# Norm factors and bank scaling ahead in the order, attention scores as 64-row products, and 14 operand tiles, in a four-layer decoder kernel

## The chip, the cores and the metric

The kernel runs as one program on one core of a Trainium2 chip. The metric is device microseconds for one execution. TensorE (PE in the rows, its weight loads PEld) does the products, VectorE (DVE) and ScalarE (ACT) the work on elements, GpSimd (POOL) a few additions and fills, and SyncE (SP) issues the transfers. Weights come from HBM in transfers of 1 MB and are used once.

## The reference

The input is one sequence of 256 tokens with 1024 features. Four layers each add three sublayers to it: a feed-forward, a mixer, a feed-forward. The mixer is differential attention in layers 0 and 3, a recurrence (RWKV-7) in layer 1 and attention with a window of 128 tokens in layer 2. Cut to what matters here:

```
for i in range(DEPTH):                      # 4
    sh1, sc1, g1, sh2, sc2, g2, sh3, sc3, g3 = split(silu(c) @ ada_w[i] + ada_b[i])
    h = rms_norm(x, norm_g[i, 0]) * (1 + sc1) + sh1
    x = x + 0.5 * g1 * swiglu(h, ffn_w_in[i, 0], ffn_w_out[i, 0])     # 1024 -> 2 x 2816 -> 1024
    h = rms_norm(x, norm_g[i, 1]) * (1 + sc2) + sh2
    x = x + g2 * mixer(h)
    h = rms_norm(x, norm_g[i, 2]) * (1 + sc3) + sh3
    x = x + 0.5 * g3 * swiglu(h, ffn_w_in[i, 1], ffn_w_out[i, 1])
# attention of both kinds: heads of 64 features
q = rms_norm(q, q_norm_g); k = rms_norm(k, k_norm_g)
s = einsum(q, k) * 64 ** -0.5, masked
```

In differential attention 8 heads hold two score maps each; with the window, 16 query heads share 2 key heads, and two query heads are worked at a time.

## The kernel before

Activations lie with features on the 128 partitions and tokens along the row, so x is 8 tiles of 128x256. Every large product is made of three products of parts (`mm3`): weights and activations are split into a high part (`hi`) and a remainder (`lo`); line 287 multiplies high by high, 288 high weights by the activations' remainder, 289 the weights' remainder by high activations. `load` takes a 1 MB weight unit and splits it in 4 chunks: ACT casts `hi` (line 269), DVE subtracts `lo` (line 271). Beside this DVE works out the modulation vectors of later sublayers in pieces (`ada_unit`, line 344).

The instructions are handed to a scheduler that places them in one fixed order for each engine, by priority (what is written earlier comes earlier) and by its estimate of what is ready. At run time each engine goes through its order and waits where an operand or a buffer is missing.

**From one sublayer to the next.** `residual` writes a feature tile of x (line 577); `stat_add` adds up squares for the norm, and `pre` makes `xh`, the tile times its modulation scale but without the norm factor, split in two parts like every operand. `first_units` (line 519) lets PE begin with products of `xh`: a column of modulation shifts is appended to it, so that a bank of PSUM then holds the raw product in its columns 0 to 255 and the shift's product in column 256. A feed-forward does so for three weight units in six banks (tags a, d, b, two each), differential attention for three units in a, b, c, the window's attention for two in a, b. Meanwhile `rsqrt` (line 385) makes the norm factor `rsq` on DVE: a transpose (393), small steps of a Newton iteration (402 to 418), a transpose back (424). It is also used for the norms of q and k and of the heads' outputs, where the second transpose (`fin`) is called later. Then `make_h` makes the eight normalised operands `h`: `xr` (DVE, line 511), the high part (ACT, 513), the remainder (DVE, 514). `unraw` (line 536) finishes a bank of the raw start: ACT copies the shift's column, DVE multiplies the bank by `rsq` (line 541) and so frees it. `xh` and `h` share one ring of 10 tiles (tag h of pool `hp`), of which 8 hold `xh` until PE is through with them.

PSUM has two banks for each of the tags a, b, c, d. In a feed-forward, the unit after the raw ones goes to banks d and the next to a, so PE needs both freed.

**Scores.** `scores` (line 764) fills two banks for a head (or for two query heads of the window), c = 0 and 1. A mask product writes the bank (line 776), then queries 0 to 127 against keys 0 to 127 (777) and queries 128 to 255 against all 256 keys (779) are added. The two maps of a head lie on partitions 0 to 63 and 64 to 127 of q and k. Each product takes all 128 partitions: q is held twice in a padded tile `qp`, once with the lower and once with the upper half zero. The zeros are written once (`zero_tiles`), the 64 rows by two ACT instructions for each head (lines 906 and 1027), which also multiply by the q norm's gain. Keys are multiplied by the k norm's gain and norm factor (line 911, in the window 1071). There are 24 calls of `scores`: 8 in each differential layer and 8 in the window's.

Of the kernel before, what the change touches and what calls it, by code (L numbers as in the profile page):

```python
# [19 lines left out]
P = 128  # L20
# [208 lines left out]
class Trunk:  # L229
    def __init__(self, tc, ctx, aps, plan):  # L230
# [6 lines left out]
        self.hp = e(tc.tile_pool(name="hp", bufs=10))  # L237
# [147 lines left out]
    def rsqrt(self, ps, n, scale, eps, pool, floor=None, later=False, more=None):  # L385
# [41 lines left out]
        return fin if later else fin()  # L427
# [175 lines left out]
    def ffn(self, l, s):  # L603
# [4 lines left out]
        with ExitStack() as c:  # L608
# [16 lines left out]
            for j in range(first, NPAIR + 1):  # L625
                if j == 5:
                    self.load_rest()
                if j < NPAIR:
# [7 lines left out]
                    g = hp.tile([P, 2, 2, T], F32R, tag="g", bufs=NFIRST + 1 if first else 2, name=self.n("g"))  # L636
# [65 lines left out]
    def first_pairs(self, l, s, hp):  # L702
# [7 lines left out]
        for kp in range(4):  # L710
# [20 lines left out]
            for i in range(2):  # L731
# [5 lines left out]
                for k, j, f, c in todo:  # L737
# [8 lines left out]
                    if kp == 3 and (k, f, c) == (1, 1, 1):  # L746
                        gs[2 * i + j] = self.glu(hp, *banks[2 * i + j], bufs=NFIRST + 1)
# [16 lines left out]
    def scores(self, qp, kn, window):  # L764
# [5 lines left out]
        banks = []  # L770
        for c in range(2):
            ps = self.ps("a")
            b3 = ps[:, :384].rearrange("p (b k) -> p b k", b=3)
            mk = self.msk[:, P:].rearrange("p (b k) -> p b k", b=3)
            st = 1 if window else 2
            nc.tensor.matmul(b3[:, ::st], self.msk[:, :P], mk[:, ::st], start=True, stop=False, skip_group_check=True)
# [84 lines left out]
    def diff(self, l):  # L861
# [4 lines left out]
        with ExitStack() as c:  # L866
            mp = c.enter_context(self.tc.tile_pool(name=self.n("da"), bufs=2))
            qpads = self.zero_tiles(mp, [P, 2, T], "qp", 3)
# [25 lines left out]
            def head(h, qs, ks, raw):  # L894
                if raw:
                    sb = mp.tile([P, 512], F32, tag="qk", bufs=2, name=self.n("qk"))
# [618 lines left out]
```

## Time and profile before

| | |
|---|---|
| median of 3 runs | 2309.99 us (2307.81 to 2311.01) |
| the profiled execution's own time | 2310.26 us |
| its span, first to last instruction | 2308.4 us |
| mean granted TensorE clock | 0.974 |
| PE busy | 2193.9 us, 95% |
| PEld busy | 2104.0 us, 91% |
| DVE busy | 1766.9 us, 77% |
| ACT busy | 1196.4 us, 52% |

The profiled execution lies 0.27 us above the median and has 1.9 us outside its span. Windows give for a stretch of the span each engine's busy time and instructions, and the granted clock: 1.00 is 2.4 GHz, 0.50 is 1.2 GHz, a value between them a mixture of both. A timeline lists an engine's instructions with their start; equal neighbours stand as one row with a count (x3). The duration of a matmul overlaps the next one's, so what a matmul costs in a row of them is the distance between starts.

### The profile page before, as it was taken

What the parts mean: (1) busy time and instruction counts of PE and PEld (TensorE: products, weight loads), DVE (VectorE), ACT (ScalarE), POOL (GpSimd) and SP (SyncE); (2) the same over time, 40 slices, a digit from 0 to 9 for tenths busy, and PEclk for the clock granted to TensorE, in tenths of its full rate; (3) what the DMA queues carried; (4) which work ended last, traced back from release to release, by engine and by line L of the source; (5) the groups of instructions that cost most, each with busy time, mean ns of one, the idle gap of its engine ahead of it and who ended that gap; (6) DMA issues with size and microseconds to landing.
All of it is one profiled execution on the core that took longest, in us unless ns stands there. A gap on an engine that the chain in (4) does not pass through costs nothing.

```text
span 2308.4 us, 47699 instructions
## 1 busy us (share of the span) xinstructions
PE 2193.9 (95%) x19244; PEld 2104.0 (91%) x19244; DVE 1766.9 (77%) x4001; ACT 1196.4 (52%) x2675; POOL 112.7 (5%) x213
## 2 busy tenths in 40 slices
PE   7999899999999899888999999999999999999999
PEld 6999898999999687677999899888999999889999
DVE  6877999888855776767888965778889855999653
ACT  3545766445444474445444644586445444766442
POOL 0001001001000300001000100101001000101000
PEclk8999999999999998899999999999999999999999
DMA  8885456887754420026788665436888755554552
GB/s 341 357 330 207 176 190 243 341 328 289 277 183 183 148 74 2 21 74 239 285 317 329 261 249 183 157 146 231 338 321 305 282 183 183 185 190 158 201 183 74
DMA packets 72365, 505.90 MB, mean 219 GB/s; under 512 B 8016, under 2 KB 10448, under 8 KB 11600
## 3 DMA queue, kind: packets, MB, share of 16 engines
q1 hardware_dynamic: 71568, 502.20, 57.6%
q8 instruction: 151, 2.47, 0.4%
q10 hardware_dynamic: 576, 0.66, 0.1%
q14 instruction: 70, 0.57, 0.1%
HBM read 501.78 MB, written 1.05 MB: 218 GB/s over the span
## 4 chain that ended last, share of the span: by engine, by line
PE 45%; DVE 5%; ACT 1%; issue 1%; POOL 0%; DVEq 0%; ACTq 0%; POOLq 0%
PE psa L287 4%; PE psa L289 4%; PE psa L288 4%; PE psd L287 4%; PE psd L289 4%; PE psd L288 4%; PE psb L288 3%; PE psb L287 3%; PE psb L289 3%; PE psc L288 2%; PE psc L289 2%; PE psc L287 2%; DVE lo L271 2%; DVE x L577 1%; DVE xh L490 1%
## 5 line engine op out<-in xcount | busy, mean ns | idle before, releaser
L269 ACT CAST hi<-raw 128x512 fp32r<-128x512 f32 x1306 | 731.3, 618 | 720.2 <-issue 553.5
L271 DVE TENSOR_TENSOR lo<-raw,hi 128x512 fp32r<-128x512 f32 x1306 | 847.3, 691 | 240.2 <-ACT hi L269 239.3
L287 PE MATMUL psa<-h,hi 128*128 128x256 f32 x1336 | 377.7, 283 | 29.3 <-DVE sil L541 23.8
L289 PE MATMUL psa<-h,lo 128*128 128x256 f32 x1336 | 377.3, 282 | 0.0
L288 PE MATMUL psa<-h,hi 128*128 128x256 f32 x1336 | 376.8, 282 | 0.0
L287 PE MATMUL psd<-h,hi 128*128 128x256 f32 x1256 | 359.0, 286 | 0.0
L289 PE MATMUL psd<-h,lo 128*128 128x256 f32 x1256 | 359.0, 286 | 0.0
L288 PE MATMUL psd<-h,hi 128*128 128x256 f32 x1256 | 358.4, 285 | 0.0
L344 DVE SCALAR_TENSOR_TENSOR ada<-ada,cb 128x1024 f32<-128x1024 f32 x232 | 276.3, 1219 | 27.1 <-DMA ada<-in_ada_dram 27.1
L287 PEld LDWEIGHTS psa<-h,hi 128*128 128x128 f32 x1336 | 255.0, 191 | 31.1 <-ACT hi L269 17.3
L288 PEld LDWEIGHTS psa<-h,hi 128*128 128x128 f32 x1336 | 253.0, 189 | 0.2
L289 PEld LDWEIGHTS psa<-h,lo 128*128 128x128 f32 x1336 | 252.9, 189 | 0.0
L287 PEld LDWEIGHTS psd<-h,hi 128*128 128x128 f32 x1256 | 243.7, 194 | 0.7
L288 PEld LDWEIGHTS psd<-h,hi 128*128 128x128 f32 x1256 | 242.4, 193 | 0.7 <-issue 0.7
L289 PEld LDWEIGHTS psd<-h,lo 128*128 128x128 f32 x1256 | 242.0, 193 | 0.3
L289 PE MATMUL psb<-g,lo 128*128 128x256 f32 x704 | 199.3, 283 | 0.0
L287 PE MATMUL psb<-g,hi 128*128 128x256 f32 x704 | 199.3, 283 | 0.0
L288 PE MATMUL psb<-g,hi 128*128 128x256 f32 x704 | 199.2, 283 | 0.0
L288 PE MATMUL psc<-g,hi 128*128 128x256 f32 x704 | 199.0, 283 | 0.0
L289 PE MATMUL psc<-g,lo 128*128 128x256 f32 x704 | 199.0, 283 | 0.0
L287 PE MATMUL psc<-g,hi 128*128 128x256 f32 x704 | 198.9, 283 | 0.0
L289 PEld LDWEIGHTS psb<-g,lo 128*128 128x128 f32 x704 | 135.0, 192 | 0.0
(373 smaller groups left out, 4464.4 us busy)
## 6 DMA issues: line engine op xcount, KB each, us to landing
raw<-in_ffi_dram SPq DMA_DIRECT2D x175, 1024.0 KB, 4.9
ada<-in_ada_dram SPq DMA_DIRECT2D x116, 1024.0 KB, 7.3
raw<-in_ffo_dram SPq DMA_DIRECT2D x88, 1024.0 KB, 4.9
raw<-in_ada_dram SPq DMA_DIRECT2D x24, 1024.0 KB, 4.8
raw<-in_daqk_dram SPq DMA_DIRECT2D x16, 1024.0 KB, 4.8
raw<-in_rwr_dram SPq DMA_DIRECT2D x12, 1024.0 KB, 4.8
raw<-in_ff_dram SPq DMA_DIRECT2D x8, 1024.0 KB, 9.6
raw<-in_dav_dram SPq DMA_DIRECT2D x8, 1024.0 KB, 4.8
```

Of the source, the lines that this page charges most:

```text
L269: nc.scalar.copy(hi[:, sl], raw[:, sl])
L271: eng.tensor_tensor(lo[:, sl], raw[:, sl], hi[:, sl].bitcast(F32), op=ALU.subtract)
L287: nc.tensor.matmul(out, whi, ahi, start=start, stop=False, skip_group_check=True)
L288: nc.tensor.matmul(out, whi, alo, start=False, stop=False, skip_group_check=True)
L289: nc.tensor.matmul(out, wlo, ahi, start=False, stop=stop, skip_group_check=True)
L344: nc.vector.scalar_tensor_tensor(wk, wk, 1.0, self.cond, op0=ALU.mult, op1=ALU.mult, accum_out=raw[:, k:k + 1])
L490: nc.vector.scalar_tensor_tensor(h[:, 1, :T], self.x[d], a[:, d:d + 1], h[:, 0, :T].bitcast(F32), op0=ALU.mult, op1=ALU.subtract)
L577: nc.vector.scalar_tensor_tensor(t, acc[d // 2][:, (d % 2) * T:(d % 2 + 1) * T], gate[:, d:d + 1], self.x[d], op0=ALU.mult, op1=ALU.add)
```

## The change

It has four parts.

1. `rsqrt` and its `fin`, and the two instructions of `unraw`, are issued under `tc.high_priority()`: the scheduler places them ahead of other work that is ready.
2. `scores` takes q without padding. The product of map c uses partitions 64c to 64c + 63 of q and of the keys, so each product is 64 rows deep. The order in which they are written is: mask 0, mask 1, the two products of 128 keys, the two of 256 keys. The gain of q goes into the keys (`qkg`, one product of two vectors for each layer). The padded tiles, their fills and the two ACT copies for each head go. Where q came out of a raw bank (3 of 8 heads in a differential layer, 2 of 8 calls in the window's) the tile `qk` is used as it is; elsewhere one ACT copy of 128x256 takes it out of PSUM. `qk` has 3 buffers in the differential layers in place of 2.
3. The ring of tag h has 14 tiles in place of 10.
4. The ring of tag g in the program's first feed-forward has NFIRST tiles in place of NFIRST + 1 (NFIRST counts the pairs of hidden blocks with which the program begins).

```diff
-        self.hp = e(tc.tile_pool(name="hp", bufs=10))
+        self.hp = e(tc.tile_pool(name="hp", bufs=14))
...
-    def rsqrt(self, ps, n, scale, eps, pool, floor=None, later=False, more=None):
+    def rsqrt(self, *args, later=False, **kw):
+        with self.tc.high_priority():
+            fin = self._rsqrt(*args, **kw)
+        def done():
+            with self.tc.high_priority():
+                return fin()
+        return done if later else done()
+    def _rsqrt(self, ps, n, scale, eps, pool, floor=None, more=None):
...
-        nc.scalar.copy(b, bank[:, T:T + 1])
-        nc.vector.tensor_tensor(out, bank[:, :T], self.rs, op=ALU.mult)
+        with self.tc.high_priority():
+            nc.scalar.copy(b, bank[:, T:T + 1])
+            nc.vector.tensor_tensor(out, bank[:, :T], self.rs, op=ALU.mult)
...
-        banks = []
+        banks = [self.ps("a") for _ in range(2)]
+        b3 = [ps[:, :384].rearrange("p (b k) -> p b k", b=3) for ps in banks]
...
         for c in range(2):
...
-            nc.tensor.matmul(ps[:, 0:128], qp[:, c, 0:128], kn[:, 0:128], start=False, stop=True,
-                             skip_group_check=True)
-            nc.tensor.matmul(ps[:, 128:384], qp[:, c, 128:256], kn, start=False, stop=True, skip_group_check=True)
-            nc.vector.tensor_reduce(m3[:, c], b3, axis=AX.X, op=ALU.max)
-            banks.append(ps)
+            nc.tensor.matmul(b3[c][:, ::st], self.msk[:, :P], mk[:, ::st], start=True, stop=False, skip_group_check=True)
+        for qs, ks in ((slice(0, P), slice(0, P)), (slice(P, T), slice(0, T))):
+            for c in range(2):
+                r = slice(c * 64, c * 64 + 64)
+                os = slice(0, P) if qs.start == 0 else slice(P, 3 * P)
+                nc.tensor.matmul(banks[c][:, os], q[r, qs], kn[r, ks], start=False, stop=True, skip_group_check=True)
...
-                qp = qpads[h % 3]
-                for cc in range(2):
-                    ps_ = slice(cc * 64, cc * 64 + 64)
-                    nc.scalar.activation(qp[ps_, cc], qs[ps_], AF.Copy, scale=self.v("daqg", j)[ps_])
+                if not raw:
+                    q = mp.tile([P, T], F32, tag="q", bufs=3, name=self.n("q"))
+                    nc.scalar.copy(q, qs)
+                    qs = q
...
-                nc.vector.scalar_tensor_tensor(kn, ks, self.v("dakg", j), rk, op0=ALU.mult, op1=ALU.mult)
+                nc.vector.scalar_tensor_tensor(kn, ks, qkg, rk, op0=ALU.mult, op1=ALU.mult)
...
-                banks, mx = self.scores(qp, kn, False)
+                banks, mx = self.scores(qs, kn, False)
```

What the scheduler makes of it is seen in three places. In the excerpts a row is line, operation, out<-in and size; the number behind a name is that tile's own, and the changed kernel's lines stand 11 to 16 further down in this part (541 becomes 553, 511 becomes 522, 514 becomes 525, 424 becomes 435).

**DVE at the start of layer 2's last feed-forward**, from the transpose back of the norm factor (rsq) on. Before:

```order
L424 STREAM_TRANSPOSE rsq_15604<-ry_15592 128x256
L271 TENSOR_TENSOR lo_15926<-raw_15923,hi_15925 128x512
L511 SCALAR_TENSOR_TENSOR xr_15606<-x_15385,mod_14026,rsq_15604 128x256
...
L514 SCALAR_TENSOR_TENSOR h_15608<-xr_15606,mod_14020,h_15608 128x256
...
L511 SCALAR_TENSOR_TENSOR xr_15621<-x_15428,mod_14026,rsq_15604 128x256
...
L514 SCALAR_TENSOR_TENSOR h_15623<-xr_15621,mod_14020,h_15623 128x256
...
L511 SCALAR_TENSOR_TENSOR xr_15641<-x_15487,mod_14026,rsq_15604 128x256
L541 TENSOR_TENSOR sil_15528<-psa_15542,rsq_15604 128x256
L541 TENSOR_TENSOR gf_15529<-psd_15544,rsq_15604 128x256
L541 TENSOR_TENSOR sil_15528<-psa_15543,rsq_15604 128x256
L514 SCALAR_TENSOR_TENSOR h_15643<-xr_15641,mod_14020,h_15643 128x256
```

After:

```order
L435 STREAM_TRANSPOSE rsq_15594<-ry_15582 128x256
L271 TENSOR_TENSOR lo_15916<-raw_15913,hi_15915 128x512
L553 TENSOR_TENSOR sil_15518<-psa_15532,rsq_15594 128x256
L553 TENSOR_TENSOR gf_15519<-psd_15534,rsq_15594 128x256
L553 TENSOR_TENSOR sil_15518<-psa_15533,rsq_15594 128x256
L553 TENSOR_TENSOR gf_15519<-psd_15535,rsq_15594 128x256
L553 TENSOR_TENSOR sil_15799<-psb_15536,rsq_15594 128x256
L522 SCALAR_TENSOR_TENSOR xr_15596<-x_15375,mod_14016,rsq_15594 128x256
...
L553 TENSOR_TENSOR sil_15799<-psb_15537,rsq_15594 128x256
L525 SCALAR_TENSOR_TENSOR h_15598<-xr_15596,mod_14010,h_15598 128x256
...
L522 SCALAR_TENSOR_TENSOR xr_15611<-x_15418,mod_14016,rsq_15594 128x256
```

The five bank products that stood behind eight `xr` and seven `h` (line 541, four are shown) now stand right behind the transpose, ahead of the first `xr`, and a sixth (the last unit's second bank) behind the third `xr`.

**PE at the same place**: the last products of `xh`, then the first of `h`. Before:

```order
L289 MATMUL psb_15547<-xh_15491,lo_15533 128x258
L287 MATMUL psa_15974<-h_15608,hi_15925 128x256
L287 MATMUL psd_15811<-h_15608,hi_15786 128x256
L288 MATMUL psd_15811<-h_15608,hi_15786 128x256
L289 MATMUL psd_15811<-h_15608,lo_15787 128x256
...
L287 MATMUL psd_15811<-h_15613,hi_15786 128x256
```

After:

```order
L289 MATMUL psb_15537<-xh_15481,lo_15523 128x258
L287 MATMUL psd_15801<-h_15598,hi_15776 128x256
L287 MATMUL psa_15964<-h_15598,hi_15915 128x256
L288 MATMUL psd_15801<-h_15598,hi_15776 128x256
L289 MATMUL psd_15801<-h_15598,lo_15777 128x256
...
L287 MATMUL psd_15801<-h_15603,hi_15776 128x256
...
L288 MATMUL psa_15964<-h_15598,hi_15915 128x256
L289 MATMUL psa_15964<-h_15598,lo_15916 128x256
```

The first two products have changed places. Behind them PE went through both halves of unit d with each `h` in turn before (48 products ahead of the next of bank a); now the products of bank a begin to be mixed in after 17 of bank d.

**PE at the second call of `scores` in the window's attention** (psa are the score banks, psb the bank of a q projection that runs meanwhile). Before:

```order
L287 MATMUL psb_18460<-h_17945,hi_18274 128x256
L776 LDWEIGHTS msk
L776 MATMUL psa_18344<-msk 128x384
L777 MATMUL psa_18344<-kns_18187,qp_17843 128x128
L779 MATMUL psa_18344<-kns_18187,qp_17843 128x256
L288 MATMUL psb_18460<-h_17945,hi_18274 128x256
L289 MATMUL psb_18460<-h_17945,lo_18275 128x256
L287 MATMUL psb_18460<-h_17950,hi_18274 128x256
L776 LDWEIGHTS msk
L776 MATMUL psa_18349<-msk 128x384
L777 MATMUL psa_18349<-kns_18187,qp_17843 128x128
L779 MATMUL psa_18349<-kns_18187,qp_17843 128x256
```

After, where line 787 is the mask and 792 both score products:

```order
L288 MATMUL psb_18440<-h_17949,hi_18254 128x256
L787 LDWEIGHTS msk
L787 MATMUL psa_18324<-msk 128x384
L792 MATMUL psa_18324<-kns_18167,qk_18036 128x128
L792 MATMUL psa_18324<-kns_18167,qk_18036 128x256
L289 MATMUL psb_18440<-h_17949,lo_18255 128x256
L287 MATMUL psb_18440<-h_17954,hi_18254 128x256
L288 MATMUL psb_18440<-h_17954,hi_18254 128x256
L787 LDWEIGHTS msk
L787 MATMUL psa_18325<-msk 128x384
L792 MATMUL psa_18325<-kns_18167,qk_18036 128x128
L792 MATMUL psa_18325<-kns_18167,qk_18036 128x256
```

Here the products of the two maps have stayed apart: each map's two follow its own mask, with products 128 rows deep between. The scheduler has left 13 of the 24 calls in this form. In 8 calls the four 64-row products stand together, as in this one of layer 0:

```order
L287 MATMUL psb_2817<-h_2586,hi_2451 128x256
L792 MATMUL psa_2844<-kn_2769,qk_2697 128x128
L792 MATMUL psa_2845<-kn_2769,qk_2697 128x128
L792 MATMUL psa_2844<-kn_2769,qk_2697 128x256
L792 MATMUL psa_2845<-kn_2769,qk_2697 128x256
L288 MATMUL psb_2817<-h_2586,hi_2451 128x256
```

There nothing stands between the two maps' products. In the other 3 calls the two products of a head's output (lines 939 and 940 before) stand somewhere between the four.

Over the whole program PE has the same number of instructions; DVE has 3 more, POOL 10 fewer, and ACT 32 fewer (48 copies of 64x256 become 16 of 128x256).

## Rows read from the trace of the kernel before

**Rows 1.** The page's first part: busy time, share of the span and instructions of each engine.

```profile
PE 2193.9 (95%) x19244; PEld 2104.0 (91%) x19244; DVE 1766.9 (77%) x4001; ACT 1196.4 (52%) x2675; POOL 112.7 (5%) x213
```

**Rows 2.** The waits of PE by what released them: what waited, for whom, us in total, times, longest in us.

```profile
PE psa L287 <- DVE sil L541: 23.8, 6, 4.5
...
PE psa L776 <- DVE qk L541: 6.0, 2, 3.5
...
PE psa L776 <- ACT hi L269: 4.7, 2, 3.8
```

**Rows 3.** Windows of 12 us from the end of the raw products of each feed-forward that has them (the last row is the seventh, in layer 3): us, then PE, PEld, DVE, ACT and POOL busy (instructions), the granted clock, the share of DMA, GB/s.

```profile
380.00:392.00 12.00, 8.32 (x59) 8.14 (x58) 11.34 (x26) 8.03 (x17) 0.00 (x0) 0.86 0.32 122
579.00:591.00 12.00, 8.40 (x51) 8.19 (x50) 11.65 (x25) 6.60 (x16) 0.00 (x0) 0.72 0.28 96
1097.00:1109.00 12.00, 7.54 (x42) 7.47 (x42) 11.97 (x28) 8.01 (x17) 0.00 (x0) 0.72 0.27 107
1296.00:1308.00 12.00, 7.99 (x53) 7.67 (x52) 12.00 (x28) 6.71 (x16) 0.00 (x0) 0.86 0.32 117
1592.00:1604.00 12.00, 7.94 (x46) 7.72 (x46) 11.98 (x28) 8.03 (x18) 0.00 (x0) 0.72 0.47 168
1791.00:1803.00 12.00, 7.96 (x49) 7.73 (x48) 12.00 (x27) 6.71 (x16) 0.00 (x0) 0.72 0.31 114
2130.00:2142.00 12.00, 12.00 (x103) 12.00 (x102) 12.00 (x28) 10.82 (x23) 0.00 (x0) 1.00 0.21 72
```

**Rows 4.** Timeline of DVE at one of them, layer 2's last feed-forward: start, us, line, operation, out<-in.

```profile
1287.35 1.22 DVE L344 SCALAR_TENSOR_TENSOR ada<-ada,cb 128x1024 f32<-128x1024 f32 x1
...
1293.11 0.43 DVE L424 STREAM_TRANSPOSE rsq<-ry 128x256 f32<-128x256 f32 x1
...
1294.05 1.26 DVE L511 SCALAR_TENSOR_TENSOR xr<-x,mod,rsq 128x256 f32<-128x256 f32 x3
...
1296.42 1.66 DVE L511 SCALAR_TENSOR_TENSOR xr<-x,mod,rsq 128x256 f32<-128x256 f32 x4
1298.00 1.66 DVE L514 SCALAR_TENSOR_TENSOR h<-xr,mod,h 128x256 fp32r<-128x256 f32 x4
1299.59 0.47 DVE L511 SCALAR_TENSOR_TENSOR xr<-x,mod,rsq 128x256 f32<-128x256 f32 x1
1299.98 0.41 DVE L541 TENSOR_TENSOR sil<-psa,rsq 128x256 f32<-128x256 f32 x1
1300.32 0.41 DVE L541 TENSOR_TENSOR gf<-psd,rsq 128x256 f32<-128x256 f32 x1
```

**Rows 5.** Timeline of PE at the same place; the bracket is the idle time before the instruction and what ended it.

```profile
1296.25 0.28 PE L289 MATMUL psb<-xh,lo 128*128 128x258 f32 x1
1300.54 0.36 PE L287 MATMUL psa<-h,hi 128*128 128x256 f32 x1 [4.01 <-DVE sil L541]
...
1302.24 0.41 PE L287 MATMUL psd<-h,hi 128*128 128x256 f32 x1
1302.45 0.41 PE L288 MATMUL psd<-h,hi 128*128 128x256 f32 x1
```

**Rows 6.** Timeline of PE at a call of `scores` in the window's attention, without the mask (each fp32 product is two records), and the product behind it.

```profile
1508.52 0.38 PE L777 MATMUL psa<-kns,qp 128*128 128x128 f32 x2
1508.74 0.60 PE L779 MATMUL psa<-kns,qp 128*128 128x256 f32 x2
1509.18 0.38 PE L777 MATMUL psa<-kns,qp 128*128 128x128 f32 x2
1509.40 0.60 PE L779 MATMUL psa<-kns,qp 128*128 128x256 f32 x2
1509.64 0.47 PE L289 MATMUL psb<-h,lo 128*128 128x256 f32 x1
```

**Rows 7.** Timeline of PE in the recurrence: one product 64 rows deep (line 1245) among those of 128 rows.

```profile
854.12 0.28 PE L287 MATMUL psd<-h,hi 128*128 128x256 f32 x1
854.33 0.70 PE L1245 MATMUL psb<-lr,lw 64*128 64x256 f32 x2
854.96 0.39 PE L288 MATMUL psd<-h,hi 128*128 128x256 f32 x1
855.18 0.29 PE L289 MATMUL psd<-h,lo 128*128 128x256 f32 x1
```

**Rows 8.** Timeline of PE there where two such products, on the two halves of the rows, stand together.

```profile
923.22 0.70 PE L1245 MATMUL psb<-lr,lw 64*128 64x256 f32 x4
923.85 0.33 PE L1336 MATMUL psc<-hi 64*64 64x64 f32 x4
```

**Rows 9.** Windows of the three attentions' heads (columns as in rows 3): layers 0, 2 and 3.

```profile
244.00:380.00 136.00, 130.62 (x974) 123.61 (x973) 126.87 (x441) 92.53 (x244) 10.75 (x22) 0.98 0.56 203
1497.00:1573.00 76.00, 75.85 (x579) 67.92 (x579) 57.71 (x193) 63.91 (x182) 4.75 (x11) 1.00 0.39 140
1996.00:2118.00 122.00, 113.97 (x839) 106.24 (x838) 110.62 (x399) 80.83 (x217) 9.44 (x21) 0.97 0.50 182
```

**Rows 10.** Groups of ACT by line and shape: out<-in, count, busy us, mean ns, idle before: a copy into a padded tile, and a whole copy out of PSUM of the shape that the new copy of q has.

```profile
L906 ACT ACTIVATE qp<-psb,vec 64x256 f32<-64x256 f32 x20 | 9.4, 469 | 0.2
...
L942 ACT COPY on<-psd 128x256 f32<-128x256 f32 x16 | 5.9, 370 | 11.2 <-PE psd L940 11.1
```

More of the change, by code (lines that the diff above doesn't have):

```diff
@@ L425, in fin @@
             return r if more is None else (r, y[:, nk:])
-        return fin if later else fin()
+        return fin
     def stat_begin(self):
@@ L635, in ffn @@
                     self.ada(k)
-                    g = hp.tile([P, 2, 2, T], F32R, tag="g", bufs=NFIRST + 1 if first else 2, name=self.n("g"))
+                    g = hp.tile([P, 2, 2, T], F32R, tag="g", bufs=NFIRST if first else 2, name=self.n("g"))
                     sil = hp.tile([P, 512], F32, tag="sil", bufs=2, name=self.n("sil"))
@@ L761, in glu, with scores @@
         return g
-    def scores(self, qp, kn, window):
+    def scores(self, q, kn, window):
         nc = self.nc
@@ L769, in scores @@
         mx = self.sm.tile([P, 2, 2], F32, tag="mx", bufs=3, name=self.n("mx"))
-        banks = []
+        banks = [self.ps("a") for _ in range(2)]
+        b3 = [ps[:, :384].rearrange("p (b k) -> p b k", b=3) for ps in banks]
+        mk = self.msk[:, P:].rearrange("p (b k) -> p b k", b=3)
+        st = 1 if window else 2
         for c in range(2):
[L772 to L776, printed above, removed]
-            nc.tensor.matmul(ps[:, 0:128], qp[:, c, 0:128], kn[:, 0:128], start=False, stop=True,
-                             skip_group_check=True)
-            nc.tensor.matmul(ps[:, 128:384], qp[:, c, 128:256], kn, start=False, stop=True, skip_group_check=True)
-            nc.vector.tensor_reduce(m3[:, c], b3, axis=AX.X, op=ALU.max)
-            banks.append(ps)
+            nc.tensor.matmul(b3[c][:, ::st], self.msk[:, :P], mk[:, ::st], start=True, stop=False, skip_group_check=True)
[4 more added lines that the diff above has]
+                nc.tensor.matmul(banks[c][:, os], q[r, qs], kn[r, ks], start=False, stop=True, skip_group_check=True)
+        for c in range(2):
+            nc.vector.tensor_reduce(m3[:, c], b3[c], axis=AX.X, op=ALU.max)
         nc.vector.tensor_copy(mx[:, 0], m3[:, :, 0])
@@ L867, in diff @@
             mp = c.enter_context(self.tc.tile_pool(name=self.n("da"), bufs=2))
-            qpads = self.zero_tiles(mp, [P, 2, T], "qp", 3)
+            qkg = self.sm.tile([P, 1], F32, tag="qkg", name=self.n("qkg"))
+            nc.vector.tensor_tensor(qkg, self.v("daqg", j), self.v("dakg", j), op=ALU.mult)
             self.load_rest()
@@ L895, in head @@
                 if raw:
-                    sb = mp.tile([P, 512], F32, tag="qk", bufs=2, name=self.n("qk"))
+                    sb = mp.tile([P, 512], F32, tag="qk", bufs=3, name=self.n("qk"))
                     for i, b in enumerate((qs, ks)):
@@ L988, in slide @@
             mp = c.enter_context(self.tc.tile_pool(name=self.n("sw"), bufs=2))
-            qpads = self.zero_tiles(mp, [P, 2, T], "qp", 4)
+            qkg = self.sm.tile([P, 1], F32, tag="qkg", name=self.n("qkg"))
+            nc.vector.tensor_tensor(qkg, self.v("swqg"), self.v("swkg"), op=ALU.mult)
+            qt = {}
             self.load_rest()
@@ L1023, in pads @@
             def pads(ft, q):
-                qp = qpads[ft % 4]
-                for hh in range(2):
-                    ps_ = slice(hh * 64, hh * 64 + 64)
-                    nc.scalar.activation(qp[ps_, hh], q[ps_], AF.Copy, scale=self.v("swqg")[ps_])
+                if ft > 1:
+                    qt[ft] = mp.tile([P, T], F32, tag="q", bufs=4, name=self.n("q"))
+                    nc.scalar.copy(qt[ft], q)
+                else:
+                    qt[ft] = q
             def heads(ft, r8):
                 g = ft // 4
-                banks, mx = self.scores(qpads[ft % 4], kns[0][:, g], True)
+                banks, mx = self.scores(qt[ft], kns[0][:, g], True)
                 s = mp.tile([P, 2, 384], F32, tag="s", bufs=2, name=self.n("s"))
@@ L1162, in rwkv @@
                                                            op1=ALU.mult)
-                        ms.append(self.split(self.hp, "h", 10, mixed(i, d)))
+                        ms.append(self.split(self.hp, "h", 14, mixed(i, d)))
                     if i == 2:
@@ L1443, in tile_gen @@
             nc.vector.tensor_tensor(oo, oo, pb[:, T:], op=ALU.mult)
-            outs.append(self.split(self.hp, "h", 10, oo))
+            outs.append(self.split(self.hp, "h", 14, oo))
         rkv.append(self.slab("raw", (P, ND, T)))
```

4 lines of the change are left out of this document (2 added, 2 removed).

## The prediction

> **What bounds the kernel now.** I read the busy shares first: PE is busy 95% of the span, DVE 77%, ACT 52% [rows 1]. So the end is set by PE's work, and a change pays where PE waits or runs slowly, or where it shortens or lengthens PE's own products. The waits of PE come next. The largest single releaser that the change touches is the scaling of the raw banks: six waits, 23.8 us, the longest 4.5 [rows 2]. These are the starts of feed-forwards behind raw products, one per start. Two more kinds belong to it: the score banks' wait for the same scaling at attention entries (6.0 us, two times, 3.5 at most) and for a weight cast at another (4.7, two times, 3.8 at most) [rows 2].
>
> The windows at the starts show what such a wait costs beyond its idle time. Six of seven starts get 59, 51, 42, 53, 46 and 49 matmuls done in 12 us, 300 in all; the seventh, without a wait, gets 103 at a granted clock of 1.00 [rows 3]. The six are short of 6 x 103 by 318 matmuls. One takes 12.00/103 = 0.1165 us, so the starts lose 37.0 us: 23.8 of waiting, and some 13 because the clock fell behind the gap. It is 0.72 or 0.86 in those windows [rows 3]; behind the wait at 1300.54 neighbouring products stand 0.21 us apart (1302.24 and 1302.45), which is the lower level [rows 5].
>
> Why PE waits is seen on DVE. PE's last raw product starts at 1296.25 and its next at 1300.54 [rows 5]. The norm factor's transpose back starts at 1293.11, but DVE first makes eight xr and seven remainders of h, and the first bank is scaled only at 1299.98 [rows 4]; DVE is busy 11.3 to 12.0 of the 12 us [rows 3]. PE goes on 0.15 us after that scaling ends. The bank, not h, ends this wait.
>
> **Starts of feed-forwards (priority, 14 tiles).** In the new order the bank scalings stand right behind the transpose. I lay the rows' durations along it. The transpose and one weight remainder take from 1293.11 to 1294.05. Five scalings at 0.34 (1299.98 to 1300.32) end at 1295.75; three xr at 0.395 ((1298.00 - 1296.42)/4) at 1296.9; the sixth scaling at 1297.3; the first remainder of h 0.4 later, at 1297.7 [rows 4]. PE has ended its raw products at 1296.4, so it waits to about 1297.8, some 1.4 us in place of 4.0. One piece of modulation work fewer stands within the Newton steps (1.22 us [rows 4]), but the sixth scaling needs the last raw bank, so little of that arrives: 1.2 us at best. The third h is there at 1298.5, then come four xr and the fourth h at 1300.5. With the products of bank a mixed in, PE has 23 products to do on three h, 2.7 us, and reaches the fourth at 1300.5 as well; from there each h takes 0.4 us of DVE and feeds six products, 0.7 us. So I expect one gap of 1.2 to 1.5 us and no second. I take 1.5, which is 9.0 us for six starts, and gain 37.0 - 9.0 = 28.0 us. The seventh start has no wait to lose.
>
> Bounds: 37.0 if nothing remains. At the other end the clock falls behind the shorter gap too and costs what it does now, 13/6 = 2.2 us for each start; with about 1.3 us of idle time that is 6 x 3.5 = 21 lost, and 16 gained.
>
> The ring of 14 is what allows the order: with 10, eight are held by xh until PE is done, and only two h can be written ahead. I put no gain of its own on it. It costs no instruction. The ring of g in the first feed-forward has one tile less; that stretch's order is unchanged, and I count nothing, as its tiles are taken one after another by products that PE does in any case.
>
> **Entries of the attentions.** The same scaling moves ahead of weight remainders at the three entries. What waits there now is 3.8, 3.5 and 6.0 - 3.5 = 2.5 us [rows 2]. As the scalings also delay h, I keep about 0.8, 0.5 and 1.0 of these and gain 3, 3 and 1.5: 7.5 us (bounds 0 and 11). The recurrence's entry and the heads' later norms get their factors a little earlier and the weight remainders a little later; I count 0, with 6 us gained to 4 lost for the differential layers, where PE is idle 136.00 - 130.62 = 5.4 and 122.00 - 113.97 = 8.0 us [rows 9].
>
> **Scores.** Before, the two products of one map take 1509.18 - 1508.52 = 0.66 us, those of a call 1.32 [rows 6]. Products 64 rows deep on the two halves run side by side: a pair takes 923.85 - 923.22 = 0.63 us [rows 8], a single one 854.96 - 854.33 = 0.63 [rows 7]. But going from 128 rows to 64 and back costs time: the stretch from 854.12 to 855.18 is 1.06 us [rows 7], where two large products (0.1165 each) and one score product of 256 keys (0.44, 1508.74 to 1509.18 [rows 6]) would take 0.67. A round trip costs 0.39, say 0.4. So a call whose four products stand together takes 0.66 + 0.40, a gain of 0.26. A call left apart saves nothing and makes two round trips, a loss of 0.80. The order has 8 of the first, 13 of the second, and 3 that are split, for which I take one further round trip, 0.40. By stage: the window's attention has 1 and 7, +5.3; layer 0 has 3, 3 and 2 split, +2.4; layer 3 has 4, 3 and 1 split, +1.8. Sum +9.5. In the window PE is busy 75.85 of 76 us [rows 9], so all 5.3 counts. In the differential layers PE has idle time, and I count 1.2 of 4.2. Together +6.5, bounds +9.5 and, were the round trip free, 8 x 0.66 + 3 x 0.33 = -6.3.
>
> ACT loses 48 copies of 469 ns and gains 16 of about 370 [rows 10], some 16 us in all. None lies on the path at 52% busy, except that q and its norm come a little earlier; 0. The fills on POOL and the extra small products on DVE: 0, since they are off the path and made once in a layer.
>
> **The sum.** 2310.26 - 28.0 - 7.5 + 6.5 = 2281.3 us for the profiled execution, which is 0.27 above the median of the runs; 2281.
>
> **Rivals.**
> A: the switch is hidden. The weight load of the next product might cover the change of mode. Then the scores give -6.3 and the time is 2310.26 - 28.0 - 7.5 - 6.3 = 2268.5. For it: PE often has other work in its queue; against it: rows 7, where large products stood on both sides and the time was still lost. Chance 0.12. The Trainium skill, page "TensorEngine Tiling (Array Packing)", section "Theoretical Speedup", is on this rival's side: it gives up to 2x for a contraction of 64 or less. By it all 24 calls would save half, 24 x 0.66 = 15.8 us, and the sum would be 2259; 13 calls left apart can't pair, so I hold that inside this rival's chance. Its section "Key Properties" says that a change of the tiling mode drains TensorE and names no price, which the trace gives as 0.39 us [rows 6, 7].
> B: the wait comes back in part. The scalings delay every h by six times 0.34, 2.0 us, DVE is full at the starts [rows 3], and the weight remainders that were put back are then late; gaps in two places of a start let the clock fall as it does now. Half of the gain at the starts goes: 2310.26 - 14.0 - 7.5 + 6.5 = 2295. Chance 0.20.
> C, slower: the wait only changes its name. It was for a bank, and becomes one for the first remainder of h. That decides where this remainder ends at about 1300.4 and not 1297.7, so if 2.7 us of other DVE work stand ahead of it. Then the starts and entries gain nothing, the switches cost their 9.5, and the time is 2319.8. For it: 11.3 to 12.0 of 12 us busy on DVE [rows 3], and a queue in which anything that waits holds up what follows; the sixth scaling does wait for PE. Against it: the order shows three xr and six scalings ahead of the first h, no more. Chance 0.08.
> D, no change: the starts as in B, nothing at the entries, the whole 9.5: 2305.8. Chance 0.06.
>
> **How the numbers follow.** Forecast 0.54. About 0.2% (4.6 us) is what a measurement can tell from no change. Faster are the forecast, A and B: 0.86; D is 0.06 the same, C 0.08 slower. The range for 8 in 10: downwards past A, with a further 6 us that the differential layers may give back, 2263; upwards past B, with the scores' whole 9.5 and the 4 us on the differential layers, 2303. C, D and the tails beyond the ends are left out.
>
> **What would show it.** In the profile after, the waits for the scaling should fall from 23.8 us to under 10 (now named for the scaling or for h), the windows at the starts should hold 85 to 95 matmuls at a clock near 1.00. If they hold 70 at 0.8, B is right; if 50, C. In the window's attention the four score products should be found 0.8 us longer for a call left apart, and its stage about 5 us longer; if it is not longer, A is right. The forecast is wrong if another wait of more than 10 us in sum appears that the table of before does not have, above all for a weight remainder.

## The result and the profile after

The changed kernel takes 2276.01 us (median of 4 runs, 2274.46 to 2279.0), beside 2310.5 us for the kernel before in the same comparison: 0.9852 of its time, 95% interval 0.9835 to 0.9869, 34.5 us less. The forecast was 2281 with a range of 2263 to 2303. The profiled execution took 2279.0 us with a span of 2277.1, so between the two profiled executions lie 31.3 us, and the sum had 29.0.

The page of the changed kernel, part 1 (for [rows 1]):

```profile
PE 2190.4 (96%) x19244; PEld 2087.9 (92%) x19244; DVE 1756.9 (77%) x4004; ACT 1176.1 (52%) x2643; POOL 111.9 (5%) x203
```

PE and DVE do as many instructions as forecast, and PE's share has gone up a little. DVE's bank scalings [rows 2] are in the table of waits no more; their copy on ACT is there once, with 0.5 us. Of what that table has now that is new or larger (columns as in rows 2):

```profile
PE psc L287 <- ACT o L561: 9.0, 3, 4.0
PE psc L478 <- POOL ssum L463: 7.9, 5, 2.0
...
PE psd L288 <- DVE h L525: 3.1, 4, 0.9
```

The windows at the starts of the seven feed-forwards (columns as in [rows 3], each from the end of the raw products):

```profile
377.50:389.50 12.00, 12.00 (x99) 11.74 (x99) 12.00 (x26) 8.79 (x20) 0.00 (x0) 1.00 0.25 89
572.00:584.00 12.00, 11.08 (x91) 10.82 (x91) 11.32 (x24) 8.88 (x19) 0.00 (x0) 1.00 0.19 58
1085.75:1097.75 12.00, 11.01 (x88) 10.47 (x88) 12.00 (x28) 10.13 (x24) 0.00 (x0) 1.00 0.39 132
1282.50:1294.50 12.00, 11.16 (x92) 10.86 (x91) 11.66 (x25) 9.00 (x20) 0.00 (x0) 1.00 0.24 86
1576.25:1588.25 12.00, 12.00 (x100) 11.77 (x99) 12.00 (x27) 8.95 (x20) 0.00 (x0) 1.00 0.25 91
1771.00:1783.00 12.00, 11.22 (x91) 10.87 (x91) 11.65 (x26) 8.93 (x20) 0.00 (x0) 1.00 0.23 81
2101.00:2113.00 12.00, 12.00 (x101) 11.84 (x100) 12.00 (x25) 8.82 (x20) 0.00 (x0) 1.00 0.44 157
```

The first six hold 99, 91, 88, 92, 100 and 91 matmuls, 561 in place of 300, and the granted clock is 1.00 in all. 618 - 561 = 57 are short, 6.6 us by the 0.1165 of the prediction. The starts recover 261 x 0.1165 = 30.4 us.

PE at the same start as in [rows 5]:

```profile
1282.59 0.28 PE L289 MATMUL psb<-xh,lo 128*128 128x258 f32 x1
1282.70 0.36 PE L287 MATMUL psd<-h,hi 128*128 128x256 f32 x1
1282.90 0.28 PE L287 MATMUL psa<-h,hi 128*128 128x256 f32 x1
1284.02 0.39 PE L288 MATMUL psd<-h,hi 128*128 128x256 f32 x1 [0.84 <-DVE h L525]
1284.25 0.28 PE L289 MATMUL psd<-h,lo 128*128 128x256 f32 x1
```

The wait is 0.84 us in place of 4.01, and it is for the first remainder of h. DVE there (compare [rows 4]):

```profile
1279.01 0.44 DVE L435 STREAM_TRANSPOSE rsq<-ry 128x256 f32<-128x256 f32 x1
1279.37 0.65 DVE L271 TENSOR_TENSOR lo<-raw,hi 128x512 fp32r<-128x512 f32 x1
1279.94 0.41 DVE L553 TENSOR_TENSOR sil<-psa,rsq 128x256 f32<-128x256 f32 x1
...
1281.27 0.41 DVE L553 TENSOR_TENSOR sil<-psb,rsq 128x256 f32<-128x256 f32 x1
1281.60 1.26 DVE L522 SCALAR_TENSOR_TENSOR xr<-x,mod,rsq 128x256 f32<-128x256 f32 x3
1283.15 0.42 DVE L553 TENSOR_TENSOR sil<-psb,rsq 128x256 f32<-128x256 f32 x1 [0.29 <-ACT ub L552]
1283.49 1.26 DVE L525 SCALAR_TENSOR_TENSOR h<-xr,mod,h 128x256 fp32r<-128x256 f32 x3
```

The five scalings follow the transpose and one weight remainder, three xr come next, the sixth scaling waits for PE's last raw bank by way of ACT's copy, and the first remainder starts at 1283.49. The prediction laid out just this row of work, and made the wait 0.6 us too long (1.4).

To see where the 31.3 us come from, the span is cut at the last raw product of each sublayer (before: 239.74, 379.99, 579.08, 1096.78, 1296.25, 1487.41, 1592.30, 1790.98, 1989.60 and 2132.53 us; after: 239.74, 377.44, 572.05, 1085.68, 1282.59, 1469.41, 1576.38, 1770.95, 1964.13 and 2101.05). A feed-forward's piece holds its start, since this lies behind its raw products. Pieces in us for the kernel before, and the difference from it for the others (kernels of the next section; cut in the same way in their traces):

| piece | before | changed | padded scores, 10 tiles (e1) | products together (e6) | all apart (e9) | residual first (e10) |
|---|---|---|---|---|---|---|
| up to the first attention | 239.74 | 0.0 | -0.4 | -0.7 | -1.5 | -2.2 |
| attention, layer 0 | 140.25 | -2.5 | -2.7 | -6.6 | +0.2 | -3.9 |
| feed-forward, end of layer 0 | 199.09 | -4.5 | -3.4 | -4.9 | -2.9 | -7.3 |
| feed-forward and recurrence, layer 1 | 517.71 | -4.1 | -6.6 | -5.5 | -11.2 | -12.4 |
| feed-forward, end of layer 1 | 199.47 | -2.6 | -2.6 | -2.7 | -0.8 | -4.5 |
| feed-forward, layer 2 | 191.16 | -4.3 | -4.7 | -4.1 | -4.1 | -4.4 |
| window's attention, layer 2 | 104.88 | +2.1 | -4.3 | -0.7 | +4.8 | +0.2 |
| feed-forward, end of layer 2 | 198.69 | -4.1 | -5.6 | -5.7 | -5.7 | -6.5 |
| feed-forward, layer 3 | 198.62 | -5.4 | -5.0 | -5.4 | -5.4 | -6.0 |
| attention, layer 3 | 142.93 | -6.0 | -5.4 | -8.6 | -1.5 | -4.7 |
| last feed-forward | 175.87 | +0.2 | +0.1 | +0.2 | 0.0 | +0.3 |
| span | 2308.4 | -31.3 | -40.5 | -44.5 | -28.0 | -51.4 |

Each column is one execution. A second trace of the changed kernel (e5) has the same pieces within 0.3 us, but for 0.8 in layer 0's attention. The execution profiled is the slowest of the changed kernel's four (2279.0 us) and the fastest of e9's and e10's (2282.22 and 2258.85), so the bottom line is no measure of a kernel; the medians below are.

In the changed kernel the six pieces with a waiting start give 4.5 + 4.1 + 2.6 + 4.3 + 4.1 + 5.4 = 25.0 us (forecast 28.0); the second of these, 4.1, lies in the recurrence's piece, which moves by more than that from kernel to kernel. So 5.4 of the 30.4 us recovered within 12 us are lost again later in the same pieces, nearly all of it in two: the start of layer 1's last feed-forward recovers 46 matmuls, 5.4 us, and its piece keeps 2.6; that of layer 2's last recovers 54, 6.3 us, and its piece keeps 4.1. PE at the end of the first of them, before and in the changed kernel:

```profile
1281.06 0.70 PE L467 MATMUL psc<-ssum,ones 128*128 128x256 f32 x2 [0.55 <-POOL ssum L452]
```

```profile
1264.40 0.28 PE L289 MATMUL psd<-xh,lo 128*128 128x258 f32 x1
1266.69 0.91 PE L478 MATMUL psc<-ssum,ones 128*128 128x256 f32 x2 [2.02 <-POOL ssum L463]
...
1267.62 0.42 PE L288 MATMUL psa<-xh,hi 128*128 128x258 f32 x1
1267.83 0.42 PE L289 MATMUL psa<-xh,lo 128*128 128x258 f32 x1
```

PE waits 2.02 us in place of 0.55 for the sum of squares that the next norm factor needs, and behind it neighbouring products stand 0.21 us apart, the lower clock level. At the end of layer 2's feed-forward the same wait goes from 0.56 to 2.00 us (1775.83 before, 1755.05 after). In both places DVE now has a modulation piece between the last feature tiles of x:

```profile
1260.91 0.47 DVE L589 SCALAR_TENSOR_TENSOR x<-psc,mod,x 128x256 f32<-128x256 f32 x1
1261.31 1.21 DVE L344 SCALAR_TENSOR_TENSOR ada<-ada,cb 128x1024 f32<-128x1024 f32 x1
...
1263.32 0.47 DVE L589 SCALAR_TENSOR_TENSOR x<-psb,mod,x 128x256 f32<-128x256 f32 x1
```

Before, no such piece stood there, and two stood behind the sum, beside the Newton steps (one of them at 1287.35 [rows 4]). At the end of layer 0's feed-forward a piece stands among the tiles in both kernels, PE waits 2.02 and 2.00 us, and little is lost by the change. All traces of the next section without the residual's priority agree: at these three ends the wait is 2.0 us where a piece stands ahead of the sum and 0.55 where none does. So the new order has moved a piece from behind the sum to ahead of it at two of the ends.

The attentions of layers 0 and 3 give something back too, at their output projection (layer 0):

```profile
347.73 0.28 PE L289 MATMUL psb<-o,lo 128*128 128x256 f32 x1
351.80 0.50 PE L287 MATMUL psc<-o,hi 128*128 128x256 f32 x2 [3.80 <-ACT o L561]
...
352.67 0.42 PE L289 MATMUL psc<-o,lo 128*128 128x256 f32 x1
352.88 0.41 PE L287 MATMUL psc<-o,hi 128*128 128x256 f32 x1
```

PE has come to the last head's output 3.80 us early, as the projections that lay in front are done. Before, the largest such wait was 1.2 us.

### The profile page after: what moved, and what is told of

Its sections match the earlier page's. It is cut to its first block, busy times and chain, and to the rows that moved or that the text cites. A ratio compares the mean times of both kernels' runs of the same rounds, so it can differ in the third digit from the quotient of the medians.

```text
span 2277.1 us, 47510 instructions
## 1 busy us (share of the span) xinstructions
PE 2190.4 (96%) x19244; PEld 2087.9 (92%) x19244; DVE 1756.9 (77%) x4004; ACT 1176.1 (52%) x2643; POOL 111.9 (5%) x203
## 4 chain that ended last, share of the span: by engine, by line
PE 53%; DVE 7%; ACT 2%; issue 1%; DMA 1%; POOL 0%; DVEq 0%; SPq 0%; ACTq 0%; POOLq 0%
PE psa L288 4%; PE psa L289 4%; PE psa L287 4%; PE psd L288 4%; PE psd L289 4%; PE psd L287 4%; PE psb L287 4%; PE psb L288 4%; PE psb L289 4%; PE psc L288 3%; PE psc L287 3%; PE psc L289 3%; DVE lo L271 2%; PE psa L792 1%; PE psc L1353 1%
## 5 line engine op out<-in xcount | busy, mean ns | idle before, releaser
L288 PE MATMUL psd<-h,hi 128*128 128x256 f32 x1256 | 355.3, 283 | 3.1 <-DVE h L525 3.1
L287 PE MATMUL psd<-h,hi 128*128 128x256 f32 x1256 | 354.4, 282 | 0.5 <-ACT ub L552 0.5
L288 PEld LDWEIGHTS psd<-h,hi 128*128 128x128 f32 x1256 | 237.0, 189 | 4.9 <-DVE h L525 3.9
L287 PEld LDWEIGHTS psd<-h,hi 128*128 128x128 f32 x1256 | 239.3, 191 | 1.4 <-ACT ub L552 0.7
L289 PEld LDWEIGHTS psd<-h,lo 128*128 128x128 f32 x1256 | 236.9, 189 | 0.3
L288 PEld LDWEIGHTS psb<-g,hi 128*128 128x128 f32 x704 | 135.2, 192 | 0.0
```

The lines of the kernel that those rows point to most:

```text
L287: nc.tensor.matmul(out, whi, ahi, start=start, stop=False, skip_group_check=True)
L288: nc.tensor.matmul(out, whi, alo, start=False, stop=False, skip_group_check=True)
L289: nc.tensor.matmul(out, wlo, ahi, start=False, stop=stop, skip_group_check=True)
```

## The experiments

Each was timed beside the kernel before. One caution holds for all: single runs of the kernel before lie between 2301.5 and 2315.7 us in these comparisons, and the piece with the recurrence, whose code hardly changes, moves by 8 us between kernels (4.1 to 12.4 in the table), with different amounts of time at the lower clock (granted 0.95 on the mean in the changed kernel, 0.97 in e10). Differences of 3 us between two kernels are not told from nothing; the pieces above say more.

**e1: the priorities alone.** The `rsqrt` and `unraw` parts of the diff on the kernel before; against the changed kernel:

```diff
-        self.hp = e(tc.tile_pool(name="hp", bufs=14))
+        self.hp = e(tc.tile_pool(name="hp", bufs=10))
...
-                banks, mx = self.scores(qs, kn, False)
+                banks, mx = self.scores(qp, kn, False)
```

> The kernel before with the two priorities alone (norm factors and bank scalings), 10 operand tiles, padded scores. Theory (the priority does all of the gain, the scores' mode changes cost what the order adds, of which the window's 5.3 us and perhaps 1 us of the rest are on the path, the ring adds nothing): 6 to 7 us under the changed kernel, about 2270 us. Rival 1 (the 14 tiles are needed for the new order to pay, since with 10 only two h can be written while xh is held): at 2283 us or more. Rival 2 (all 9.5 us of the mode changes are on the path): 2266.5 us.

2268.83 us (2267.51 to 2269.77), 0.9825 of before, interval 0.9806 to 0.9844. Rival 1 falls: the order pays with 10 tiles. The theory's 2270 and rival 2's 2266.5 lie too close together for this scatter; the pieces speak for the theory. Without 64-row products the window's attention gains 4.3 us instead of losing 2.1, so they cost 6.4 us there. In the differential layers they cost nothing that can be seen (-2.7 and -5.4 against -2.5 and -6.0). As a whole the 64-row products and the 14 tiles make the kernel slower than the priorities alone.

**e2: 10 tiles.**

The changed kernel with that diff's part on the ring, at all its places, and with the ring of g as before the change.

> The changed kernel with 10 operand tiles instead of 14 (and the g ring as before). Theory: the ring carries nothing, 2276 us within 3. Rival 1: h waits for tiles that xh holds at each of six starts, some 1 to 2 us each, with the clock falling in some of them: 2283 to 2290 us.

2272.23 us (2269.8 to 2275.06), interval of the ratio 0.9822 to 0.9863. So the larger ring is not needed. With the changed kernel timed once more (e5) and the pair e6 and e7 the 14 tiles came out 3 us longer both times, which the scatter does not separate from zero, and no piece is shorter by more than 0.6 us with 10 tiles in both pairs; a gain from 14 is not seen.

**e3: no priority.** The changed kernel without both parts:

```diff
-        with self.tc.high_priority():
-            fin = self._rsqrt(*args, **kw)
+        fin = self._rsqrt(*args, **kw)
...
-        with self.tc.high_priority():
-            nc.scalar.copy(b, bank[:, T:T + 1])
-            nc.vector.tensor_tensor(out, bank[:, :T], self.rs, op=ALU.mult)
+        nc.scalar.copy(b, bank[:, T:T + 1])
+        nc.vector.tensor_tensor(out, bank[:, :T], self.rs, op=ALU.mult)
```

> The changed kernel without either priority: 64-row scores and 14 tiles alone. Theory: the waits for the bank scalings come back at six starts (20 to 25 us) and the scores' cost stays: 2310.5 plus 6 to 9, so 2316 to 2320 us. Rival 1: 14 tiles alone give back a part of the starts, since h can be written earlier: 2300 us or less.

2312.08 us (2308.68 to 2315.64), ratio 1.001, interval 0.9999 to 1.0021. All the gain is gone, and the scalings' waits are back (waits of PE):

```profile
PE psa L287 <- DVE sil L541: 24.5, 7, 4.1
...
PE psa L775 <- DVE qk L541: 8.6, 4, 3.9
```

The loss against the kernel before is smaller than the expected 6 to 9: 1.75 us. The window's attention loses 6.7, but the differential layers gain 0.8 and 2.4 and the rest scatters. One reason is in PE's order: without the priorities the scheduler keeps 13 of the 24 calls of `scores` together and leaves 11 apart, 6 and 2 in each differential layer, so that by the prediction's prices they cost 5.4 us in place of 9.5.

**e4 and e8: one priority each.** e4 has the first half of the diff of e3 (no priority for `rsqrt` and `fin`), e8 the second (none for `unraw`).

> The changed kernel with the priority on the bank scalings alone; the norm factors are issued as before. Theory: the starts depend on where the scalings stand behind the factor, so nearly all of the gain stays: 2276 to 2280 us. Rival 3: the factor's own earlier steps matter (one modulation piece of 1.2 us less ahead of it at each of 9 starts and entries, and earlier factors in the heads): 2286 us or more.

> The changed kernel with the priority on the norm factors alone; the bank scalings stand behind eight xr again. Theory (the factor's priority takes one modulation piece from ahead of the factor and shortens the heads' norms, and is worth the 6.6 us that the run without it lost): the kernel without priority, 2312, less 6 to 8: 2304 to 2306 us, with six waits for scalings of about 3 us each. Rival (the two priorities are of use together only): 2312 us.

e4 took 2282.66 us (2281.87 to 2288.18), e8 2314.41 (2311.98 to 2320.17; ratio 1.0024, interval 1.001 to 1.0038). e4 differs from e3 by the scalings' priority alone and has the same 13 calls together: it brings 29.4 us by itself (27.7 against the kernel before, with the scores' cost in it). That of the factor brings 6.6 on top of it and nothing without it. Both expectations missed: e4 lies between its 2276 to 2280 and the rival's 2286, so the factor's own place counts for more than I thought, and e8 (2304 to 2306 expected) fits its rival's 2312. But the two are not of use only together, as that rival has it: the scalings' priority works alone, the factor's does not. The waits of e8 show why:

```profile
PE psa L287 <- DVE sil L552: 20.6, 7, 4.0
...
PE psa L786 <- DVE qk L552: 8.5, 4, 3.9
```

An earlier factor does not help while eight xr stand between it and the scaling that PE waits for.

**e5: the changed kernel again.**

> The changed kernel once more, as the neighbour of the two runs that follow it: 2276 us within 3. If it comes out near 2272, the 3.8 us between it and the kernel with 10 tiles were no more than scatter; if it stays at 2276, 14 tiles cost something.

2275.05 us (2272.04 to 2280.11): the first result stands, and so do the 3 us to e2, which the scatter does not separate.

**e6 and e7: the score products kept together.** Before it, the price in the changed kernel. A map apart in the window's attention:

```profile
1491.30 0.34 PE L787 MATMUL psa<-msk 128*128 128x384 bf16 x1
1491.57 0.92 PE L792 MATMUL psa<-kns,qk 64*128 64x128 f32 x4
1492.42 0.39 PE L289 MATMUL psb<-h,lo 128*128 128x256 f32 x1
```

and a call kept together in layer 0:

```profile
250.29 0.93 PE L792 MATMUL psa<-kn,qk 64*128 64x128 f32 x8
251.15 0.39 PE L288 MATMUL psb<-h,hi 128*128 128x256 f32 x1
```

Eight records of two maps take 251.15 - 250.29 = 0.86 us, four of one map 1492.42 - 1491.57 = 0.85. So products on the two halves of the rows run side by side here where they are neighbours, and a map left apart takes as long as two together. e6 issues them so, e7 with 10 tiles as well:

```diff
         for c in range(2):
-            nc.tensor.matmul(b3[c][:, ::st], ...)
+            last = nc.tensor.matmul(b3[c][:, ::st], ...)
...
+        with self.tc.issue_after(last.ins), self.tc.high_priority():
             for qs, ks in (...):
```

> The changed kernel with the four score products of a call issued behind its second mask, so that in all 24 calls they stand together. Theory (a call left apart takes two round trips, 2 x 1.06 us in the trace, one kept together 1.05): the window's 7 calls give back 7.5 us, of which the whole is on the path there; the differential layers, which end on their heads' chain, give back under 2: 2267 to 2269 us. Rival (the products together now wait for the second bank, so the heads are later and the gain is lost): 2275 us or more.

> The same with 10 operand tiles. If the ring carries nothing: equal to the kernel with 14 tiles and products together, within 2 us. If 14 tiles cost something: 3 to 4 us under it.

2266.01 us (2265.39 to 2269.52) and 2263.09 (2259.49 to 2269.42). Products kept together are worth 10 us against the changed kernel (9 against e5), a little more than the 7 to 9 expected, but not where I expected it: the differential layers give 4.0 and 2.6 more, the window's only 2.8 of the 7.5. There PE now waits three times for softmax work on DVE and ACT, in two of them before a mask product (PE in e6):

```profile
1497.41 1.03 PE L806 MATMUL psd<-con,s 128*128 128x128 f32 x6 [1.17 <-DVE nm L1055]
1499.29 0.32 PE L787 MATMUL psa<-msk 128*128 128x384 bf16 x1 [0.85 <-ACT s L1061]
1500.46 0.48 PE L787 MATMUL psa<-msk 128*128 128x384 bf16 x1 [0.85 <-ACT s L1061]
1500.86 1.65 PE L794 MATMUL psa<-kns,q 64*128 64x128 f32 x8
1502.44 0.70 PE L1078 MATMUL psd<-pt,vs 128*64 128x256 f32 x2
```

Three gaps of 0.85 to 1.17 us, and the products behind them run at the lower clock level: the same 8 records take until 1502.44, 1.58 us and not 0.86.

**e9: all apart.** Mask 1 is issued behind map 0's products:

```diff
         for c in range(2):
+            with self.tc.issue_after(last.ins) if c else ExitStack():
                 nc.tensor.matmul(b3[c][:, ::st], ...)
...
+                    last = nc.tensor.matmul(banks[c][:, os], q[r, qs], kn[r, ks], ...)
```

> The changed kernel with the second mask issued behind the first map's two products, so that in all 24 calls the maps stand apart. Theory: the 8 calls that stood together go from 1.05 to 2.12 us and the 3 split ones up by about 0.5, 10 us on PE; the window has one of the 8 and the differential layers seven, where the trace shows PE waiting 4 us at the end for the last head, so between 2 and 8 us reach the end: 2278 to 2284 us. Rival (mode changes are hidden by the weight loads of neighbours and the gain of the run with products together came from their earlier place alone): 2276 us.

2285.51 us (2282.22 to 2286.09), 9.5 above the changed kernel: near the whole 10 that I counted on PE, and a little past the range that I gave (2278 to 2284). The three attention pieces lose 2.8, 2.7 and 4.6 us against the changed kernel. So the mode changes are not hidden.

**e10, e11 and e12: the residual first.** `residual` with its squares, sum and raw operand is put under the same priority; e10 on the changed kernel, e11 on e7, e12 on e1.

```diff
     def residual(self, acc, d, gate):
+        with self.tc.high_priority():
+            self._residual(acc, d, gate)
```

> The changed kernel with the residual, its squares, their sum and the raw operand of the next sublayer issued under the same priority. Theory (what the starts gave is in part lost again at the end of three feed-forwards, where PE waits 2.0 us for the sum of squares behind casts and a modulation piece and the clock falls for 3.4 us after it): up to 3 x 3.7 = 11 us less, 2265 to 2270 us, and the waits for the sum gone. Rival (DVE is full there, so the weight remainders come late in their place and the waits only change name): 2274 to 2280 us.

> Products together in all calls, 10 operand tiles, and the residual's chain under priority. If the two are independent: 2263 less what the run with the residual first gains over 2276; 2253 to 2263 us.

> The two priorities on the kernel before (padded scores, 10 tiles) and the residual's chain under priority. If independent of the scores: 2269 less the same amount; 2259 to 2269 us, and above the run with 64-row products together by 4 to 6 us, which is what 64-row products are worth when none stands apart.

e10 took 2263.67 us (2258.85 to 2270.28), 12 less than the changed kernel and a little more than expected. Of the waits for the sum (7.9 us, 5 times) one is left, in the program's first feed-forward:

```profile
PE psc L478 <- POOL ssum L463: 2.3, 1, 2.3
```

The feed-forward ends of layers 0, 1 and 2 give 2.8, 1.9 and 2.4 us more than in the changed kernel, 7.1 in all, of which 4.3 are at the two ends whose wait the change had lengthened; the largest part of what is left lies in the recurrence's piece, which I don't count. e11 took 2254.03 us (2251.59 to 2254.86; 0.9761 of before, interval 0.974 to 0.9782), the fastest of all, and e12 2257.47 (2256.51 to 2267.9; 2259 to 2269 expected). So the two repairs add up within the scatter, and 64-row products kept together are 3.4 us better than padded ones, a little under the 4 to 6 expected and within the scatter of e12. Without the residual's priority the same pair, e7 and e1, stands 5.7 us apart in the same direction, with runs that overlap.

## Why the prediction was right, step by step

**The bound and its place: right.** PE waited for the scaling of the raw banks and not for h. e4 shows that this scaling's place is the cause: moved alone, it brings 29.4 us against e3; e3 and e8, where it stays, bring none.

**Starts, 28.0: measured 25.0.** The gap that remains was taken as 1.5 us a start and measures 57 x 0.1165 / 6 = 1.1 us; the clock stays at 1.00 as assumed. The 30.4 us recovered exceed the forecast. What the step left out is where the scheduler puts other work in the new order: 5.4 us are given back at the other end of the sublayers, above all at the ends of layers 1 and 2, where a piece now stands ahead of the sum of squares. e10 bears this out: with the residual's chain first, these two give 4.3 us more. The 2.8 us that layer 0's end gives there were a wait that the kernel before had too.

**Scores, +9.5 on PE, +6.5 on the path: the price right, its place not.** In the window +5.3 was forecast and e1 against the changed kernel shows 6.4. Its piece, scores and entry together, was forecast at 5.3 - 3 = +2.3 and measures +2.1, which is near by luck: the scores cost more, and the entry gave more (3.5 and 0.8 us of waits there are gone). The 3 split calls were taken at +0.40 each; a call together with one more round trip would be -0.26 + 0.40 = +0.14, 0.8 us less in all. In the differential layers 1.2 was forecast and nothing is seen. That is not because products cost nothing there: together they gain 6.6 us in the two layers and apart they lose 7.3. The mixture stands where the padded products stand, although PE's count puts it 4.2 us above. The ACT copies that went (two of 469 ns for each head, with one of 370 in their place in five of eight [rows 10]) may shorten the heads' chain by as much; no run separates this.

**Differential attentions, 7.5 - 3 - 1.2 = 3.3 us of gain expected: measured 8.5.** This is the term that was mis-sized most, by 5.2, nearly all of it in layer 3 (6.0). Part of it is the entries: the step kept 0.8 and 1.0 us of their waits, and the trace after has no wait there at all. Behind the one of layer 0 the clock had also stood at 0.50 from 243.8 to 247.0 us, which the step did not count. The later gaps it put at 0 within -6 and +4. Before, the heads make PE wait seven times in layer 3 between 2018 and 2028 us, 5.6 in all, and three times in layer 0 between 273 and 278, 3.1; after, 0.3 us is left of this in layer 3, nothing in layer 0, and waits of 0.4 to 0.7 us for a copy of v are new. e4, without the factor's priority, still has 4.2 and 3.3 us of the heads' waits. But in every trace with that priority PE waits 2.4 to 4.6 us for the last head's output, and in those without it no more than 1.7 (before, e3, e4). So the factor's priority closes the waits among the heads and opens one at their end. What it gains on balance no run separates, since e4 also has more calls of `scores` together.

**The ring: wrong.** The prediction said that 14 tiles allow the order, since `xh` holds eight of ten. e1 and e2 have the same order of scalings and xr with 10, and no longer time. The first remainder of h stands behind the sixth scaling, which needs PE's last raw bank; it starts 0.9 us after the last raw product with 14 tiles (1282.59 and 1283.49) and with 10 (1280.56 and 1281.47 in e1), and by then PE is through with `xh`.

**Rival A** (mode change hidden) falls by e9. The Trainium skill, page "TensorEngine Tiling (Array Packing)", section "Key Properties", says that changing the mode drains TensorE and that tiles work independently; the trace fits both, with 0.39 us for a round trip [rows 6, 7] and 0.86 us for eight records beside 0.85 for four. That the price is a drain no run here shows. **Rival B** (half of the starts given back) falls by its own sign: the starts hold 88 to 100 matmuls at a clock of 1.00, not 70 at 0.8. Something is given back, but it is 5.4 of 30.4 us, and at the other end of the sublayers, for a sum of squares. D, whose starts are B's, falls with it. **Rival C** falls: the first remainder of h costs PE 0.84 us and not 4.

That the sum comes within 2.3 us of the profiled difference is in part luck: starts 3.0 too much and differential layers 5.2 too little offset each other.

## What to carry to other kernels

Where PE waits for a buffer, look at what stands between the value that frees it and the instruction that frees it in the freeing engine's order: moving six such instructions at each feed-forward's start, and those at the attentions' entries, brought 29 us here, and making that value earlier brought nothing until they were moved. Products on half of the rows paid here only as neighbours; when a scheduler may put anything between them, each map left alone costs a round trip of modes, so tie them together or keep the padding. After a priority has changed the order, look where the scheduler has put the other work: here a modulation piece landed ahead of the sum that the next norm factor needs.

## What was not expected of the hardware

A wait of 2.02 us was followed by products at half the rate (granted clock 0.50 from 1268 to 1270 us). In e6 the clock was at 0.50 behind three gaps of 0.85 to 1.17 us that stand close together, while single gaps of 0.8 to 0.9 us at the starts were followed by no such fall. Nor was a longer single gap in the kernel before, at the entry of layer 3's attention:

```profile
1992.31 0.28 PE L776 MATMUL psa<-msk 128*128 128x256 bf16 x1 [2.43 <-DVE qk L541]
```

The granted clock there is 1.00 from 1992 to 1998 us. So the length of the longest gap alone does not tell whether the clock falls behind it.
